# Loading the output projection's first four weight chunks ahead of the second stream's gated attention, with new load times in the planner

## The chip, the cores and the metric

The kernel runs on one NeuronCore of a Trainium2 chip. The metric is the device time of one execution in microseconds (us). TensorE multiplies matrices, VectorE and ScalarE work elementwise, GpSimd does a few small operations, and SyncE issues all the loads and stores, which 16 DMA engines carry out. In the rows these engines are PE (PEld for its weight loads), DVE, ACT, POOL and SP.

## The reference

Two transformer-like blocks follow each other on 256 tokens of width 1024, all in float32. The first block has two layers of feed-forward, token mixing and feed-forward. The second block carries two streams, the context `c` and the latent `x`, and its first layer is the place of the change:

```
yc, ctx_states = retention_gla_mixer(hc, ...)          # stream c, from zero states
y, _           = retention_gla_mixer(h, ..., ctx_states)   # stream x, from c's final states
y  = y  @ ev_w_out        # output projection, 1024 x 1024
yc = yc @ ev_w_out
x  = layer_norm(ALPHA * x  + g1  * y,  g, b)
xc = layer_norm(ALPHA * xc + cg1 * yc, g, b)
```

The mixer has two halves of 512 columns: retention with a fixed decay for each head, and gated linear attention (GLA), whose decays depend on the token. Each scans forwards and backwards. After the layer comes a multilayer perceptron for both streams, then a layer with window attention and a last perceptron.

## The kernel before

**Split products.** A float32 product is made of three matmuls: each operand is split into a rounded part (type fp32r) and the rest. For a weight chunk of 128 x 1024 numbers `wload` takes two tiles `r4` (the two parts) and one tile `f4` (the loaded chunk, 512 KB), lets SyncE load it, lets ScalarE cast it to the first part, and VectorE subtract to get the second. There are 30 `r4` tiles and 7 `f4` tiles. For the first two blocks of columns of each feed-forward of the first block, a chunk is loaded in two loads, one from the gate and one from the up matrix (`wide` with `W2`).

**The planner.** The kernel's functions do not emit instructions. They record operations in program order (`Plan.record`, line 165), with the tiles that they read and write, and a duration worked out from the shape. `Plan.schedule` (line 256) then simulates the engines and writes down an order: whenever an engine is free in the simulation, it takes the ready operation with the lowest rank (its place in program order, plus a delay for background work). That order is emitted for each engine, and on the chip each engine goes through its instructions in that order, each waiting for what it needs. So a planned duration that is wrong does not make the result wrong, but can put an instruction that has to wait ahead of one that need not.

Three rules of the planner matter here:

- A load's data is taken to be there some time after its issue (lines 402 to 405, below). Whoever depends on a load is ready from that time on. A second load into a tile which an earlier load was the first to write depends on that first load, too (line 209), although the two write different parts.
- SyncE may only take a load whose place is at most `AHEAD` = 200 operations behind the oldest operation that was not issued (line 380).
- A tile is handed out from a fixed number of slots for each tag. `can` (line 308) lets an operation take a slot out of program order only if every earlier allocation of that tag, not yet made, still has room. For this `take` adds one to the count of each of those earlier allocations; the count isn't lowered when the overtaking tile is free again.

```
if op.nbytes:
    end = avail[e] = t + 480.0
    dma_free = max(t + 1100.0, dma_free) + op.nbytes / DMA_RATE      # DMA_RATE = 360.0 bytes/ns
    fin = dma_free + 900.0
```

**The stage of the change.** `retention_gla` does the retention half for both streams, and then the GLA half: projections for both streams, and in a loop over `both` = (`c`, `x`) the scan of each. For each of two pairs of heads (`p`) and two directions (`dr`) it builds a table `E` of exponentials in an `f4` tile (matmul, then ScalarE's exponentials), multiplies queries and keys with it on VectorE (the last reader of `E` is the product for `q0`, a tile of tag `p`, in stream `x`), makes two banks of scores in `gu` tiles and two in `acc` tiles, copies them to `M` on ScalarE, and multiplies them with the values into two `acc` tiles. After stream `c`'s scan its final states go to an `f4` tile, and the gates of both streams are computed (`silu`, weight columns from 2560 on). `finish` normalizes each stream's outputs, applies the gate and splits them.

Then comes the output projection, in two halves of 512 columns (`half`, line 1811). It takes all four `acc` tiles, two for each stream. In the first half, chunk after chunk is loaded and multiplied for both streams; in the second half all four chunks are recorded first, then the products, and then layer norm and transposes. After that come the loads of the perceptron's first weights (`mlp_w`). Two `f4` tiles hold the context's residual through all of this. Gate and bias rows (`mod_...`) are computed in the background from weights in the tiles `mw` (loads from `in_ada_w` and `in_w_mod`), which VectorE sums up in the tiles `ma`.

Of the kernel before, what the change touches and what calls it, by code (L numbers as in the profile page):

```python
# [20 lines left out]
P = 128  # L21
# [5 lines left out]
ALPHA = 4.0 ** 0.25  # L27
# [14 lines left out]


class Op:
    __slots__ = ("eng", "fns", "dur", "nbytes", "deps", "succ", "allocs", "tiles", "prio", "idx", "table", "acc", "label", "rank", "cols")


class Clock:
# [3 lines left out]
    W = 4096 / 1.2  # L52
# [21 lines left out]
class Plan:  # L74
# [90 lines left out]
    def record(self, eng, fn, outs, ins, dur, nbytes=0, table=0, share=1.0):  # L165
        acc = []
        for aps, wr in ((ins, False), (outs, True)):
            for ap in aps:
                name = self.which(ap)
                if name is None:  # L170
                    continue
                tag = self.tag_of[name]
                if tag in PSUM_TAGS or tag == "dram":
                    acc.append((name, wr, 0, P, 1))
                else:
                    acc.append((name, wr, *self.region(ap)))
        last = self.ops[-1] if self.ops else None
        merge = (
            eng == "PE" and last is not None and last.eng == "PE" and last.dur + dur <= self.MERGE
            and {a[0] for a in acc if a[1]} == {a[0] for a in last.acc if a[1]}  # L180
        )
        if eng == "PE" and self.group is not None:
            merge = self.group == "all"
            self.group = "all"
        if merge:
            op = last
            op.fns.append(fn)
            op.dur += dur
            op.cols += dur * share
        else:  # L190
            op = Op()
            op.eng, op.fns, op.dur, op.nbytes, op.table = eng, [fn], dur, nbytes, table
            op.deps, op.succ, op.allocs, op.tiles, op.acc = set(), [], [], set(), []
            op.cols = dur * share
            op.idx = len(self.ops)
            op.label = self.label
            op.rank = op.idx + self.late
            self.ops.append(op)
        i = op.idx
        for name, wr, p0, p1, m in acc:  # L200
            h = self.hist.setdefault(name, [])
            for j, w2, q0, q1, m2 in h:
                if j != i and (wr or w2) and p0 < q1 and q0 < p1 and m & m2:
                    op.deps.add(j)
            if wr and name not in self.first:
                self.first[name] = i
                op.allocs.append(name)
            elif self.first.get(name, i) != i:
                op.deps.add(self.first[name])
            op.tiles.add(name)  # L210
        for a in acc:
            h = self.hist[a[0]]
            e = (i, *a[1:])
            if e not in h[-4:]:
                if a[1]:
                    h[:] = [x for x in h if not (a[2] <= x[2] and x[3] <= a[3] and (x[4] & ~a[4]) == 0 and x[0] != i)]
                h.append(e)
        op.acc.extend(acc)
# [37 lines left out]
    def schedule(self, verbose=False):  # L256
# [19 lines left out]
        ready_t = [0.0] * len(ops)  # L276
# [4 lines left out]
        dma_free = 0.0  # L281
# [55 lines left out]
        while n < len(ops):  # L337
# [13 lines left out]
            while progress:  # L351
                progress = False
                for e in self.ENGINES:
                    if avail[e] > t:
                        continue
                    admit(e, t)
                    best = None
                    for key, h in ready[e].items():
                        if not h:
                            continue  # L360

                        cand = h[0] if can(ops[h[0][1]]) else None
                        if cand is None and key:
                            for c in sorted(h)[:12]:
                                if can(ops[c[1]]):
                                    cand = c
                                    break
                            if cand is None:
                                for c in h:
                                    if can(ops[c[1]]):  # L370
                                        cand = c
                                        break
                        if cand is not None and (best is None or cand < best[0]):
                            best = (cand, key)
                    if best is None:
                        if waiting[e]:
                            heapq.heappush(events, waiting[e][0][0])
                        continue
                    (pr, i), key = best
                    if e == "SP" and i > oldest + self.AHEAD:  # L380
                        continue
                    h = ready[e][key]
                    if h[0] == (pr, i):
                        heapq.heappop(h)
                    else:
                        h.remove((pr, i))
                        heapq.heapify(h)
                    op = ops[i]
                    take(op)
                    dur = op.dur  # L390
                    if e == "ACT" and op.table and op.table != table and not (op.table == 3 and table in (1, 2)):
                        dur += 1300.0
                        table = op.table if op.table != 3 else 2
                    if e == "PE":
                        end = clock.run(t, dur, op.cols / dur)
                        dur = end - t
                    else:
                        end = t + dur
                    avail[e] = end
                    busy[e] += dur  # L400
                    fin = end
                    if op.nbytes:
                        end = avail[e] = t + 480.0
                        dma_free = max(t + 1100.0, dma_free) + op.nbytes / DMA_RATE
                        fin = dma_free + 900.0
                    seq.append(i)
                    issued[i] = True
                    while oldest < len(ops) and (issued[oldest] or ops[oldest].rank > oldest):
                        oldest += 1
                    self.start[i], self.end[i] = t, end  # L410
                    n += 1
                    heapq.heappush(events, end)
                    heapq.heappush(events, fin)
                    heapq.heappush(done, (fin, i))
                    for sx in op.succ:
                        o = ops[sx]
                        lat = (0.0 if op.nbytes else self.WRITE[e] + self.WAIT[o.eng]) if o.eng != e or op.nbytes else 0.0
                        ready_t[sx] = max(ready_t[sx], fin + lat)
                        ndep[sx] -= 1
                        if not ndep[sx]:  # L420
                            put(o)
                    progress = True
# [155 lines left out]
def two_blocks_kernel(ctx: ExitStack, tc: tile.TileContext, A: dict, out: bass.AP, dumps=None):  # L578
# [54 lines left out]
    def acc():  # L633
        return nc.tile("acc", 512, F32, 4)
# [277 lines left out]
    def kpairs(tiles):  # L912


        def f(k):
            c = slice((k % 2) * T, (k % 2) * T + T)
            return tiles[k // 2][0][:, c], tiles[k // 2][1][:, c]

        return f
# [5 lines left out]
    def kstream(tiles, n):  # L925


        def f(k):
            c = (k % 2) * 2 * T
            c = slice(c, c + 2 * T) if n is None else slice(c + n * T, c + n * T + T)  # L930
            return tiles[k // 2][0][:, c], tiles[k // 2][1][:, c]

        return f
# [568 lines left out]
    def retention_gla(nT, lgam, between):  # L1502
# [219 lines left out]
        S0 = None  # L1722
        for n in both:
            own = n == "c"
            po = [acc() for _ in range(2)]
            kd = [b2(), b2()] if own else None
            for p in range(2):
# [78 lines left out]
                S0 = states(kd, vb["c"], "g")  # L1806
                g = silu(2560)
            finish(n, po, g, ng)
        return {n: kpairs(y[n]) for n in both}

    def half(hid, W, k0, j, alpha, x, gates, tail, after=(), stats=None):


        order = [(n, t) for n in ("c", "x") for t in range(2)]
# [1 line left out]
        c = slice(j * 512, j * 512 + 512)  # L1816

        def chunk(i):
            k = (k0 + 2 * i) * P
            return wload(W[k : k + 2 * P, c].rearrange("(k p) c -> p k c", p=P), 2, 512)  # L1820

        def part(n, t, i, w):
            for k in range(2):
# [315 lines left out]
    x = {"c": hold["xc"], "x": xs}  # L2139
    both = ("c", "x")  # L2140
    nc.label = "ret"
    y = retention_gla({"c": kstream(sT, 0), "x": kstream(sT, 1), "both": kstream(sT, None)}, hold["lgam"], lambda: bg(1))

    def ln_tail(n, t, st, nxt, G, SH, g, b):
        mean, r = moments(st)
# [4 lines left out]
    get("Cg1_0", "Xg1_0")  # L2150
    gates = {n: V[n.upper() + "g1_0"] for n in both}
    stats = {(n, t): new_stats() for n in both for t in range(2)}
    half(y, A["ev_w_out_2"][0], 0, 0, ALPHA, x, gates, None, stats=stats)
    g, b = mod_row(A["ln_g_2"][0, 0]), mod_row(A["ln_b_2"][0, 0])
    nxt, maps = new_J(), {}
    for n in both:
# [128 lines left out]
```

## Time and profile before

| | |
|---|---|
| median of 3 runs | 2178.65 us (2177.21 to 2182.74) |
| the profiled execution's own time | 2175.03 us |
| its span, first to last instruction | 2173.3 us |
| busy: TensorE | 2082.8 us (96%) |
| busy: VectorE | 1592.1 us (73%) |
| busy: ScalarE | 994.3 us (46%) |
| mean granted TensorE clock, as a share of the full one | 0.986 |
| read from memory | 447.11 MB, 206 GB/s over the span |

A row of a timeline gives the start of a group of equal instructions, its length, the engine, the line, the operation with the tile written, the tiles read, sizes and the count; a bracket at its end gives how long the engine stood idle before it and what ended that. All instructions have one line, that of the recorder (L507), so they are told apart by their tiles: `f`, `r`, `b`, `p` are the tags `f4`, `r4`, `b2` and the small ones, `gu` and `acc` the accumulators. A row of a chain gives start, length, and what the time went to; a DMA there reaches from its issue to its landing.

### The profile page before, as it was taken

How to read it: one execution, taken by the hardware profiler on the slowest of the kernel's cores; microseconds unless marked ns; L12 is line 12 of the kernel's file. 1: busy time of each engine (PE TensorE's matmuls, PEld its weight loads, DVE VectorE, ACT ScalarE, POOL GpSimd, SP SyncE). 2: the span in 40 equal slices, each digit the busy share in tenths (PEclk: the TensorE clock that was granted, in tenths of full speed). 3: DMA queues.
4: the chain of work that ended last, by engine and by line, in shares of the span. 5: the costliest groups of instructions: out<-in, count | busy, mean ns of one | idle time of the engine just before them, and what ended most of it. 6: DMA issues, size and time to landing. Idle time of an engine off the chain costs nothing.

```text
span 2173.3 us, 33312 instructions
## 1 busy us (share of the span) xinstructions
PE 2082.8 (96%) x13124; PEld 1804.9 (83%) x13124; DVE 1592.1 (73%) x2115; ACT 994.3 (46%) x1527; POOL 52.4 (2%) x51
## 2 busy tenths in 40 slices
PE   7999899999999999999999899979999999999998
PEld 3899788889979998887998787768888888877997
DVE  6867898886687669899788866469754356888544
ACT  3644456454445445555544426333442331465551
POOL 0000000000000001000000000000000000000000
PEclk8999999999999999999999999999999999999999
DMA  9989867698869874686886544234742433144670
GB/s 340 369 276 322 269 207 264 223 298 272 269 224 314 260 259 149 211 264 213 277 299 229 167 149 141 87 127 140 246 156 91 137 115 102 68 156 146 204 222 30
DMA packets 273367, 450.51 MB, mean 207 GB/s; under 512 B 17677, under 2 KB 185773, under 8 KB 273209
## 3 DMA queue, kind: packets, MB, share of 16 engines
q1 hardware_dynamic: 273208, 448.37, 62.7%
q8 instruction: 103, 1.69, 0.3%
q14 instruction: 56, 0.45, 0.1%
HBM read 447.11 MB, written 1.20 MB: 206 GB/s over the span
## 4 chain that ended last, share of the span: by engine, by line
PE 66%; DVE 15%; DMA 11%; issue 3%; ACT 3%; POOL 0%; SPq 0%; DVEq 0%; ACTq 0%; POOLq 0%
PE gu L507 42%; PE acc L507 24%; DVE b L507 5%; DVE r L507 4%; DMA mw<-in_ada_w 3%; DVE ma L507 2%; DMA f<-in_ffn_wu 2%; DVE p L507 2%; ACT r L507 2%; DMA f<-in_ffn_wd 1%; DMA mw<-in_w_mod 1%; DVE resx L507 1%; DMA f<-in_w_in 1%; DMA f<-in_ev_w_out 1%; ACT b L507 1%
## 5 line engine op out<-in xcount | busy, mean ns | idle before, releaser
L507 PE MATMUL gu<-r,r 128*128 128x256 f32 (+2 forms) x8048 | 1197.8, 309 | 6.9 <-DVE r L507 3.8
L507 PEld LDWEIGHTS gu<-r,r 128*128 128x128 f32 (+1 forms) x8048 | 1093.3, 192 | 95.8 <-issue 12.0
L507 ACT CAST r<-f 128x1024 fp32r<-128x1024 f32 x545 | 564.3, 1051 | 538.8 <-PE acc L507 122.2
L507 DVE TENSOR_TENSOR r<-f,r 128x1024 fp32r<-128x1024 f32 x545 | 652.8, 1221 | 199.1 <-PE gu L507 73.2
L507 PE MATMUL acc<-r,r 128*128 128x512 f32 (+3 forms) x3264 | 724.1, 385 | 19.7 <-ACT b L507 11.6
L507 PEld LDWEIGHTS acc<-r,r 128*128 128x128 f32 (+1 forms) x3264 | 568.2, 189 | 142.8 <-ACT b L507 12.3
L507 DVE SCALAR_TENSOR_TENSOR ma<-mw,sc_all,ma 128x1024 f32<-128x1024 f32 x252 | 319.6, 1281 | 86.2 <-DMA mw<-in_ada_w 58.8
L507 ACT ACTIVATE b<-gu 128x512 f32<-128x512 f32 (+1 forms) x104 | 56.5, 554 | 143.6 <-PE gu L507 126.0
L507 DVE TENSOR_TENSOR r<-b,r 128x512 fp32r<-128x512 f32 (+1 forms) x74 | 46.0, 632 | 96.0 <-ACT r L507 95.9
L507 ACT CAST r<-gu 128x256 fp32r<-128x256 f32 (+2 forms) x130 | 42.9, 387 | 139.9 <-PE gu L507 139.9
L507 POOL TENSOR_TENSOR p<-p,mhalf 128x1 f32<-128x1 f32 (+2 forms) x42 | 49.7, 1188 | 2115.8 <-DVE p L507 2115.8
L507 PE MATMUL gu<-ident,b 128*128 128x128 f32 (+1 forms) x456 | 66.8, 292 | 33.2 <-DVE b L507 31.0
L507 PEld LDWEIGHTS gu<-ident,b 128*128 128x128 f32 (+1 forms) x456 | 49.8, 147 | 50.3 <-DVE b L507 43.4
L507 DVE TENSOR_TENSOR b<-acc,b 128x512 f32<-128x512 f32 (+1 forms) x82 | 54.9, 673 | 23.0 <-PE acc L507 21.2
L507 DVE TENSOR_TENSOR b<-b,b 128x512 f32<-128x512 f32 (+2 forms) x97 | 63.4, 667 | 6.9 <-PE acc L507 1.7
L507 ACT ACTIVATE ma<-mw,sc_all 128x1024 f32<-128x1024 f32 x36 | 41.5, 1152 | 49.1 <-DMA mw<-in_ada_w 25.6
L507 ACT ACTIVATE b<-acc,p 128x256 f32<-128x256 f32 (+1 forms) x96 | 51.5, 545 | 25.0 <-DVE p L507 20.9
L507 DVE TENSOR_TENSOR r<-gu,r 128x256 fp32r<-128x256 f32 (+2 forms) x130 | 49.5, 430 | 4.5 <-ACT r L507 4.2
L507 DVE SCALAR_TENSOR_TENSOR r<-b,r 128x512 fp32r<-128x512 f32 x44 | 30.3, 689 | 28.3 <-ACT r L507 28.1
L507 ACT CAST r<-b 128x512 fp32r<-128x512 f32 (+1 forms) x74 | 41.6, 573 | 11.8 <-DVE b L507 10.1
L507 DVE TENSOR_REDUCE p<-acc 128x2 f32<-128x512 f32 (+1 forms) x64 | 42.6, 684 | 3.3 <-PE acc L507 3.1
L507 ACT COPY b<-gu 128x512 f32<-128x512 f32 (+1 forms) x40 | 20.2, 525 | 52.0 <-PE gu L507 47.1
(122 smaller groups left out, 918.3 us busy)
## 6 DMA issues: line engine op xcount, KB each, us to landing
mw<-in_ada_w SPq DMA_DIRECT2D x128, 512.0 KB
f<-in_mlp_w SPq DMA_DIRECT2D x128, 512.0 KB
mw<-in_w_mod SPq DMA_DIRECT2D x96, 512.0 KB
f<-in_ffn_wd SPq DMA_DIRECT2D x88, 512.0 KB
f<-in_ffn_wg SPq DMA_DIRECT2D x72, 512.0 KB
f<-in_ffn_wu SPq DMA_DIRECT2D x72, 512.0 KB
f<-in_w_in SPq DMA_DIRECT2D x36, 512.0 KB
f<-in_w_gate SPq DMA_DIRECT2D x32, 512.0 KB
```

Of the source, the lines that this page charges most:

```text
L507: f(*[put(a) for a in args], **{k: put(a) for k, a in kw.items()})
```

## The change

It does three things. The first four chunks of the projection's first half (`out_chunk`) are recorded inside the GLA loop, at the start of stream `x`, and handed to `half` as `ready`. In the planner, a load into a tile that another load was the first to write, and with no overlap in what they write, is marked `soft`: it is ready when the first has been issued, not when it has landed. And the time from the end of a load's transfer to its landing is 1500 instead of 900 ns.

```diff
@@ record
             elif self.first.get(name, i) != i:
-                op.deps.add(self.first[name])
+                f = self.first[name]
+                if eng == "SP" and self.ops[f].eng == "SP" and f not in op.deps:
+                    op.soft.add(f)
+                op.deps.add(f)
             op.tiles.add(name)
+        op.soft &= op.deps
@@ schedule
                         dma_free = max(t + 1100.0, dma_free) + op.nbytes / DMA_RATE
-                        fin = dma_free + 900.0
+                        fin = dma_free + 1500.0
...
-                        ready_t[sx] = max(ready_t[sx], fin + lat)
+                        ready_t[sx] = max(ready_t[sx], end if i in o.soft else fin + lat)
@@ retention_gla
         for n in both:
             own = n == "c"
+            if not own:
+                first = [out_chunk(A["ev_w_out_2"][0], i, 0) for i in range(4)]
             po = [acc() for _ in range(2)]
...
-        return {n: kpairs(y[n]) for n in both}
+        return {n: kpairs(y[n]) for n in both}, first
+
+    def out_chunk(W, i, j):
+
+        return wload(W[2 * i * P : 2 * i * P + 2 * P, j * 512 : j * 512 + 512].rearrange("(k p) c -> p k c", p=P), 2, 512)
@@ half
-    def half(hid, W, k0, j, alpha, x, gates, tail, after=(), stats=None):
+    def half(hid, W, k0, j, alpha, x, gates, tail, after=(), stats=None, ready=None):
...
         def chunk(i):
-            k = (k0 + 2 * i) * P
-            return wload(W[k : k + 2 * P, c].rearrange("(k p) c -> p k c", p=P), 2, 512)
+            return ready[i] if ready else out_chunk(W, k0 // 2 + i, j)
@@ two_blocks_kernel
-    y = retention_gla(...)
+    y, first = retention_gla(...)
...
-    half(y, A["ev_w_out_2"][0], 0, 0, ALPHA, x, gates, None, stats=stats)
+    half(y, A["ev_w_out_2"][0], 0, 0, ALPHA, x, gates, None, stats=stats, ready=first)
```

## Rows read from the trace of the kernel before

**Rows 1.** The page, busy time of each engine, share of the span, instructions.
```profile
PE 2082.8 (96%) x13124; PEld 1804.9 (83%) x13124; DVE 1592.1 (73%) x2115; ACT 994.3 (46%) x1527; POOL 52.4 (2%) x51
```
**Rows 2.** Waits of TensorE from 1400 to 1520: total us, times, longest.
```profile
PE acc L507 <- ACT b L507: 8.8, 1, 8.8
```
**Rows 3.** Timeline of TensorE from 1310 to 1515.
```profile
1378.15 2.05 PE L507 MATMUL acc<-b,b 128*128 128x128 f32 x16 [1.60 <-DVE b L507]
...
1427.36 0.72 PE L507 MATMUL gu<-b 64*128 64x128 f32 x8 [0.84 <-DVE b L507]
...
1428.45 0.46 PE L507 MATMUL gu<-b,p 64*64 64x64 f32 x16
1437.73 2.93 PE L507 MATMUL acc<-r,r 128*128 128x512 f32 x6 [8.81 <-ACT b L507]
1440.46 1.06 PE L507 MATMUL acc<-b,b 128*128 128x128 f32 x4
...
1442.04 0.61 PE L507 MATMUL acc<-b,b 128*128 128x128 f32 x4
...
1442.85 1.64 PE L507 MATMUL acc<-r,r 128*128 128x512 f32 x6
```
**Rows 4.** Windows: length, busy by engine (count), clock, DMA share, GB/s.
```profile
1400.00:1405.00 5.00, 5.00 (x24) 4.13 (x23) 0.76 (x2) 0.66 (x2) 0.00 (x0) 1.00 0.00 0
...
1438.00:1440.00 2.00, 2.00 (x5) 1.56 (x6) 2.00 (x4) 1.67 (x2) 0.00 (x0) 0.50 0.05 20
...
1440.00:1460.00 20.00, 20.00 (x106) 17.32 (x105) 11.21 (x18) 3.54 (x7) 1.98 (x2) 0.95 0.40 114
```
**Rows 5.** Timeline of ScalarE from 1376 to 1470.
```profile
1413.11 0.60 ACT L507 ACTIVATE f<-gu 128x512 f32<-128x512 f32 x1 [0.68 <-PE gu L507]
...
1429.69 1.04 ACT L507 CAST r<-f 128x1024 fp32r<-128x1024 f32 x1 [4.23 <-DMA f<-in_ev_w_out]
...
1436.09 1.04 ACT L507 CAST r<-f 128x1024 fp32r<-128x1024 f32 x1 [4.09 <-DMA f<-in_ev_w_out]
1437.04 0.36 ACT L507 COPY b<-gu 128x256 f32<-128x256 f32 x1
...
1437.57 2.21 ACT L507 CAST r<-f 128x1024 fp32r<-128x1024 f32 x2
```
**Rows 6.** The chain that ended last, 1300 to 1520: start, us, what.
```profile
1381.49 5.67 DMA f<-in_ev_w_out
...
1428.61 7.41 DMA f<-in_ev_w_out
```
**Rows 7.** Timeline of SyncE's issues from 1340 to 1520.
```profile
1381.49 2.55 SPq L507 DMA_DIRECT2D f<-in_ev_w_out  x3
...
1417.66 9.38 SPq L507 DMA_DIRECT2D f<-in_ev_w_out  x4
...
1428.61 0.38 SPq L507 DMA_DIRECT2D f<-in_ev_w_out  x1
```
**Rows 8.** Waits of SyncE ending in 1416 to 1417.6: total us, times, longest.
```profile
SPq L507 <- DVE p L507: 21.6, 1, 21.6
```
**Rows 9.** Timeline of SyncE's issues from 0 to 70.
```profile
26.90 7.31 SPq L507 DMA_DIRECT2D f<-in_ffn_wg  x5
...
34.77 1.45 SPq L507 DMA_DIRECT2D f<-in_ffn_wu  x3
```
**Rows 10.** Timeline of TensorE from 0 to 66.
```profile
40.15 0.79 PE L507 MATMUL gu<-r,r 128*128 128x512 f32 x1 [2.24 <-ACT r L507]
42.10 9.97 PE L507 MATMUL gu<-r,r 128*128 128x512 f32 x35 [1.16 <-DVE r L507]
```
**Rows 11.** A window of the start, columns as in rows 4.
```profile
40.00:44.00 4.00, 2.69 (x6) 1.81 (x7) 4.00 (x4) 1.99 (x3) 0.00 (x0) 0.50 0.98 334
```
**Rows 12.** The chain and TensorE's timeline at the first feed-forward's end.
```profile
222.62 7.53 DMA mw<-in_ada_w
...
231.63 9.76 PE L507 MATMUL acc<-r,r 128*128 128x512 f32 x30 [4.74 <-ACT r L507]
```

More of the change, by code (lines that the diff above doesn't have):

```diff
@@ L44 @@
 class Op:
-    __slots__ = ("eng", "fns", "dur", "nbytes", "deps", "succ", "allocs", "tiles", "prio", "idx", "table", "acc", "label", "rank", "cols")
+    __slots__ = ("eng", "fns", "dur", "nbytes", "deps", "succ", "allocs", "tiles", "prio", "idx", "table", "acc", "label", "rank", "cols", "soft")
 class Clock:
@@ L193, in record @@
             op.deps, op.succ, op.allocs, op.tiles, op.acc = set(), [], [], set(), []
+            op.soft = set()
             op.cols = dur * share
@@ L2141, in two_blocks_kernel @@
     nc.label = "ret"
-    y = retention_gla({"c": kstream(sT, 0), "x": kstream(sT, 1), "both": kstream(sT, None)}, hold["lgam"], lambda: bg(1))
+    y, first = retention_gla({"c": kstream(sT, 0), "x": kstream(sT, 1), "both": kstream(sT, None)}, hold["lgam"], lambda: bg(1))
     def ln_tail(n, t, st, nxt, G, SH, g, b):
```

## The prediction

> **What bounds the kernel now.** I began with the busy shares. TensorE is busy for 2082.8 us, 96% of the span [rows 1]; only the rest, and stretches at a low clock, can be won. So the next view is what TensorE waits for. Its longest single wait, 8.8 us, is for ScalarE and lies on an accumulator of the output projection [rows 2]. The timeline shows the place. The last masks of the second stream's gated scan end at 1428.91 (1428.45 + 0.46), and the next matmul, of the projection, starts at 1437.73 [rows 3]. The reader should see three things there. The first six matmuls after the wait take 2.93 us; the same six take 1.64 us at 1442.85. The granted clock is 0.50 in 1438 to 1440 [rows 4], the lower of its two levels, 1.2 GHz, after TensorE had stood still for 8.8 us. And ScalarE did not lack input: the two copies which free the accumulators ran at 1437.04 and after, behind three casts of weight chunks, for which ScalarE waited 4.23 us and, at the last one, 4.09 us [rows 5]. ScalarE takes its instructions in the order written, so what held the copies was a load. The chain of waits names it: the load of `ev_w_out` issued at 1428.61, on its way for 7.41 us [rows 6].
>
> Why was it issued so late? Of the eight loads of this weight, three went out together from 1381.49, four between 1417.66 and 1427, and the last at 1428.61 [rows 7]. SyncE stood 21.6 us before 1417.66, waiting for a VectorE write to a `p` tile [rows 8]. In the code that is `q0`, the last reader of a gate table `E`. `can` lets a later tile overtake earlier ones of its tag only if every earlier one keeps room in the sequential order. Of the seven `f4` tiles the context residual holds two, the state matrix one and the running `E` one, so three loads may overtake the tables, and none more until they are handed out, even when the three are long done. From 1400 to 1405 DMA moved nothing, while ScalarE was busy 0.66 us of 5 and VectorE 0.76 us of 5 [rows 4].
>
> **Part 1, the four chunks.** The change records the first half's four loads, casts and subtractions ahead of the second stream's tables. They no longer overtake anything, and three loads of the second half may overtake instead. So seven of eight can be out before 1417, in the empty stretch, and one is left with the `mlp_w` loads. The four casts (1.04 us each) and four subtractions are moved, not added; they lie where ScalarE and VectorE are nearly idle. If that cover were gone they would cost at most 4 x 1.04 on ScalarE. On SyncE the four loads pass the loads of the gate rows and of one pair of `mw` tiles; those rows are first read after the scan. GpSimd issues none of these.
>
> With the last chunks in early, the copies follow the masks. How long TensorE then waits is not shown at this place; the bounds are 0 and 8.81. The nearest row is the same hand-over in the first stream's scan, 1.60 us [rows 3], and I take it: 8.81 - 1.60 = 7.2. The clock gives back 2.93 - 1.64 = 1.3 in the first six matmuls and 1.06 - 0.61 = 0.45 in the next four [rows 3]. Together 9.0 us. Does it last? From 1440 to 1460 VectorE is busy 11.21 of 20 us [rows 4], so it can take the next stage as much earlier. What is late next are the tables of the scan itself, where TensorE waited 0.84 us at most from 1419 on [rows 3].
>
> **Part 2, soft dependencies.** A second load into a tile that a load has opened is now planned when the first has been issued, not landed. That concerns the gate and up halves of the feed-forwards' first chunks, and small bias rows. At the start SyncE now issues five gate halves from 26.90 on and the first up half only at 34.77 [rows 9], so no chunk is whole before about 39. TensorE loses 2.24 and 1.16 us there [rows 10], and runs 2.69 us at the lower clock in 40 to 44 [rows 11], which costs half of that, 1.3. So the gain is at most 4.7. At the other end, VectorE is busy 4.00 of 4.00 us in that row, and DMA at 0.98 of its time, so an earlier half may only displace other work; a loss I bound by the next such wait, 4.74 at 226.89 [rows 12]. VectorE's row is the nearer one; I take a gain of 1.5.
>
> **Part 3, the load time.** The planner puts a 512 KB load's landing at 1.1 + 1.46 + 0.9 = 3.46 us after its issue on an empty queue, and now at 4.06. The chain's loads took 5.67 and 7.41 us [rows 6]. So the correction points the right way but closes only 0.6 of 2.2 to 4.0 us. No instruction is added; each order in which a cast stands near other work may flip. The wait that shows what a flip is worth is the one ending at 231.63, 4.74 us, where the chain runs through a load of 7.53 us [rows 12]. Bounds: one such wait gone, or one made elsewhere. I take 0, since 0.6 is small against 4.07 missing there. The page "SBUF — State Buffer" of the Trainium skill (section "The DMA setup-cost knee") gives a load a roughly fixed 2 us plus its bytes at an asymptote of 436 GB/s, by estimate 3.2 us here; by it the old figure was already high, this part would make the plan worse, and the late load would be worth 4.2 us less, so that the whole change gives 6.3 us and not 10.5. The trace disagrees with 5.67, 7.41 and 7.53 us, in stretches with several loads in flight.
>
> **The sum.** 9.0 + 1.5 + 0 = 10.5 us. Against the profiled execution's 2175.03 that is 2164.5. The median of the runs, 2178.65, lies 3.6 above that execution; I carry this over and predict 2168.
>
> **The rivals.**
> *The wait passes to the next load in line.* Once the projection's chunks are in, the loads of `mlp_w` take their slots, and the plan, still 1.6 us or more short, may put their casts before the copies. For it: two casts already stood between the two pairs of copies, and three of the four moved loads were early anyway. Against it: fewer loads are left after 1417, and one landing in time suffices. It gives part 2 alone, 2178.65 - 1.5 = 2177, give or take 4.7. Chance 0.20.
> *The casts come in front of the second stream's exponentials.* Those start at 1413.11 on ScalarE [rows 5] and open a chain where TensorE has little else. Three more loads may now go out just before, with their casts queued ahead. One issued before 1413.11 - 7.41 = 1405.7 is harmless; one issued at the end of the gap holds the whole scan by up to 7.41, and the clock falls again (1.75), while the old wait stays at the scan's end and the start wins nothing: 2178.65 + 9.2 = 2188. Against it: DMA is empty from 1400, so loads that may go, go early. Chance 0.11.
> *The old load time was right.* Then a cast at a change of stage is planned 0.6 too late; the kernel has eleven stages, so ten changes, 10 x 0.6 = 6.0: 2178.65 - 10.5 + 6.0 = 2174. This is what the page above would make of it. The 7.53 us load speaks against it. Chance 0.06.
> *More falls away than the one wait.* Part 2 gives its 4.7 and part 3 removes the 4.74: 2178.65 - 9.0 - 4.7 - 4.7 = 2160. Chance 0.13.
>
> **How the numbers follow.** The forecast has 0.50. About 0.3% (6.5 us) is what a measurement of this kernel can tell from no change. Faster by more: the forecast and the last rival, 0.63. Within: the first and the third, 0.26. Slower: 0.11. The range goes from the last rival's 2160 to 2180, the upper part of the first rival; it leaves out the slower case and the outer ends of the others, under 0.2.
>
> **What would show it.** Right: loads of `ev_w_out` between 1385 and 1413; no cast of them after about 1425; the wait at the projection's start under 2 us, and the clock at full level there; at the start gate and up halves alternate on SyncE, and TensorE's first feed-forward matmuls come before 40. Wrong: an 8 us wait for ScalarE still ahead of the projection, with `mlp_w` casts before it; or the exponentials waiting behind a cast; or new waits over 4 us at the ends of the feed-forwards, which would mean that the re-planned order, not the chunks, sets the result.

## The result and the profile after

| | before | after |
|---|---|---|
| median of four runs, same chip | 2180.69 us (2177.21 to 2183.47) | 2152.64 us (2148.30 to 2160.36) |
| profiled execution | 2175.03 us | 2160.36 us |
| its span | 2173.3 us | 2158.6 us |

The ratio is 0.9876, interval 0.9861 to 0.9892; the medians lie 28 us apart, where 10.5 were forecast, and the time is below the range's lower end of 2160. A reading note first: the two profiled executions lie only 14.7 us apart, since the one of before is 5.7 under its median and the one of after is the slowest of its four. So what follows finds about half of the gain in the traces, and the rest is between executions.

The page of the kernel after, its span and the busy line that answers to [rows 1].

```profile
span 2158.6 us, 33327 instructions
...
PE 2084.7 (97%) x13124; PEld 1807.8 (84%) x13124; DVE 1589.4 (74%) x2115; ACT 994.5 (46%) x1527; POOL 50.5 (2%) x51
```

The work of TensorE is the same, 13124 matmuls. Its idle time, span less busy, went from 2173.3 - 2082.8 = 90.5 us to 2158.6 - 2084.7 = 73.9. So 16.6 us of waits went, and the matmuls themselves took 1.9 us more. I use this difference as a yardstick for every kernel below; it is taken from one execution of each. What TensorE waited for over the whole span (total us, times, longest), first before:

```profile
PE gu L507 <- DVE b L507: 34.8, 26, 6.4
PE acc L507 <- ACT b L507: 11.6, 2, 8.8
PE acc L507 <- ACT r L507: 6.6, 3, 4.7
```

and after:

```profile
PE gu L512 <- DVE b L512: 32.8, 30, 6.6
...
PE acc L512 <- ACT r L512: 4.8, 2, 2.6
...
PE acc L512 <- ACT b L512: 2.6, 2, 2.3
```

The wait of the projection, 8.8 us, is the largest single one that went; the one at the first feed-forward's end, 4.7, went down too. The timeline of TensorE after shows both places, and what came new.

```profile
42.49 9.90 PE L512 MATMUL gu<-r,r 128*128 128x512 f32 x35 [2.44 <-DVE r L512]
...
228.48 0.73 PE L512 MATMUL acc<-r,r 128*128 128x512 f32 x2 [2.18 <-ACT r L512]
...
1372.93 2.98 PE L512 MATMUL acc<-b,b 128*128 128x128 f32 x16 [2.90 <-DVE b L512]
...
1422.88 0.46 PE L512 MATMUL gu<-b,p 64*64 64x64 f32 x16
1425.64 2.93 PE L512 MATMUL acc<-r,r 128*128 128x512 f32 x6 [2.30 <-ACT b L512]
1428.36 1.05 PE L512 MATMUL acc<-b,b 128*128 128x128 f32 x4
...
1431.63 1.75 PE L512 MATMUL acc<-r,r 128*128 128x512 f32 x6
```

Set the same instructions beside [rows 3]. The last masks start at 1422.88 and not 1428.45, so 5.57 us were won before the gated scan ended. The projection starts at 1425.64 and not 1437.73, 12.09 earlier, so the shorter wait (8.81 to 2.30) gave 6.5 there. The remaining 2.6 of the 14.7 us lie behind. The first six matmuls after the wait still take 2.93 us, and so the clock still fell: the windows of after (columns as in rows 4) have 0.50, as before, up to 1432.

```profile
1426.00:1428.00 2.00, 2.00 (x6) 1.52 (x6) 0.65 (x2) 0.00 (x0) 0.00 (x0) 0.50 0.19 57
1428.00:1430.00 2.00, 2.00 (x10) 1.90 (x9) 0.00 (x0) 0.00 (x0) 0.00 (x0) 0.50 0.00 0
1430.00:1432.00 2.00, 2.00 (x11) 2.00 (x10) 0.43 (x1) 0.65 (x2) 0.00 (x0) 0.53 0.00 0
1432.00:1434.00 2.00, 2.00 (x14) 1.73 (x14) 0.01 (x1) 0.00 (x0) 0.00 (x0) 1.00 0.00 0
```

At 1372.93 a wait that was 1.60 us [rows 3] is now 2.90, and the same 16 matmuls take 2.98 us and not 2.05: a piece given back.

The timeline of SyncE's issues after answers to [rows 7, 9].

```profile
28.03 0.38 SPq L512 DMA_DIRECT2D f<-in_ffn_wg  x1
28.64 0.38 SPq L512 DMA_DIRECT2D f<-in_ffn_wu  x1
...
1368.88 8.78 SPq L512 DMA_DIRECT2D f<-in_ev_w_out  x4
...
1381.77 3.54 SPq L512 DMA_DIRECT2D f<-in_ev_w_out  x3
...
1412.03 0.38 SPq L512 DMA_DIRECT2D f<-in_ev_w_out  x1
1413.77 6.82 SPq L512 DMA_DIRECT2D f<-in_mlp_w  x2
```

And that of ScalarE after to [rows 5].

```profile
1407.47 0.60 ACT L512 ACTIVATE f<-gu 128x512 f32<-128x512 f32 x1 [0.68 <-PE gu L512]
...
1423.99 1.04 ACT L512 CAST r<-f 128x1024 fp32r<-128x1024 f32 x1 [4.11 <-DMA f<-in_mlp_w]
1424.94 0.37 ACT L512 COPY b<-gu 128x256 f32<-128x256 f32 x1
```

Seven of eight chunks are out early and one is left, as the prediction said; four go out from 1368.88 and three from 1381.77, even ahead of its 1385 to 1413. The exponentials at 1407.47 wait no longer than in [rows 5]. But a cast still stands in front of the copies that free the accumulators: now one of `mlp_w`, for which ScalarE waits 4.11 us, and TensorE behind it 2.30.

### The profile page after: what moved, and what is told of

Its sections match the earlier page's. It is cut to its first block, busy times and chain, and to the rows that moved or that the text cites. A ratio compares the mean times of both kernels' runs of the same rounds, so it can differ in the third digit from the quotient of the medians.

```text
span 2158.6 us, 33327 instructions
## 1 busy us (share of the span) xinstructions
PE 2084.7 (97%) x13124; PEld 1807.8 (84%) x13124; DVE 1589.4 (74%) x2115; ACT 994.5 (46%) x1527; POOL 50.5 (2%) x51
## 3 DMA queue, kind: packets, MB, share of 16 engines
q1 hardware_dynamic: 273208, 448.37, 63.4%
## 4 chain that ended last, share of the span: by engine, by line
PE 68%; DVE 19%; DMA 7%; issue 3%; ACT 1%; POOL 1%; SPq 0%; DVEq 0%; ACTq 0%; POOLq 0%
PE gu L512 44%; PE acc L512 24%; DVE b L512 6%; DVE r L512 5%; DVE ma L512 3%; DVE p L512 2%; DMA f<-in_ffn_wu 2%; DMA mw<-in_ada_w 1%; DMA f<-in_w_gate 1%; DVE resx L512 1%; DMA f<-in_w_in 1%; ACT r L512 1%; POOL p L512 1%; DMA f<-in_w_o 0%; DVE f L512 0%
## 5 line engine op out<-in xcount | busy, mean ns | idle before, releaser
L512 ACT ACTIVATE r<-b 128x512 fp32r<-128x512 f32 x44 | 27.7, 629 | 41.1 <-DVE b L512 40.7
```

Of the source, the lines that this page charges most:

```text
L512: f(*[put(a) for a in args], **{k: put(a) for k, a in kw.items()})
```

## The experiments

The question was which part made 28 us out of 10.5. The kernels differ from the kernel before in the planner's inputs or in where the four chunks are recorded, and so in the order of the same work. Each ratio is against the kernel before on the same chip. Idle is the yardstick above (profiled execution); the last column is TensorE's wait ahead of the projection. Where I say the n-th matmul, matmuls are counted from the start of each trace, and the start of the n-th is compared; all traces have 13124.

| kernel | median us | ratio [interval] | idle us | wait us |
|---|---|---|---|---|
| before | 2180.6 to 2182.6 | 1 | 90.5 | 8.81 |
| chunks alone | 2174.50 | 0.9969 [0.9956, 0.9981] | 84.6 | 2.13 |
| soft dependencies alone | 2187.79 | 1.0026 [1.0011, 1.0040] | 100.6 | 8.98 |
| load time 1500 alone | 2155.95 | 0.9887 [0.9870, 0.9904] | 76.9 | 4.61 |
| soft and 1500, no chunks | 2154.37 | 0.9881 [0.9864, 0.9899] | 73.7 | 4.15 |
| the whole change | 2152.64 | 0.9876 [0.9861, 0.9892] | 73.9 | 2.30 |
| 1200 alone | 2167.88 | 0.9937 [0.9922, 0.9952] | 81.9 | 4.86 |
| 1490 alone | 2156.59 | 0.9889 [0.9874, 0.9904] | 75.3 | 3.90 |
| 2500 alone | 2152.28 | 0.9874 [0.9860, 0.9889] | 72.4 | 3.38 |
| 4000 alone | 2157.21 | 0.9888 [0.9872, 0.9905] | 80.9 | 0.79 |
| 1500 for `f4` chunks only | 2169.44 | 0.9945 [0.9926, 0.9963] | 84.0 | 4.71 |
| 1500 for `mw` tiles only | 2170.23 | 0.9948 [0.9930, 0.9966] | 82.5 | 8.03 |
| chunks and 2500 | 2148.37 | 0.9845 [0.9824, 0.9867] | 66.7 | 2.79 |
| whole change with 2500 | 2141.01 | 0.9815 [0.9800, 0.9830] | 63.4 | 2.94 |

**The parts, one at a time.** First the four chunks without the rest of the change.

```diff
+            if not own:
+                first = [out_chunk(A["ev_w_out_2"][0], i, 0) for i in range(4)]
...
```

> The four chunks alone, with the old load time and no soft dependencies. Theory A (the chunks carry the gain: the accumulators' copies no longer wait behind late weight casts): the wait ahead of the output projection falls from 8.8 us to about 2.3, and the kernel gains 6 to 9 us, about 2172 against 2181. Theory B (the load time carries it, at the ends of all stages): the old planned time still puts the next loads' casts ahead of the copies, the wait stays above 6 us, and the gain is under 3 us. Theory C (any edit deals the whole order anew, and the gain is the luck of one order): waits change in stages long before the edit, and the median may lie anywhere within 10 us of 2181.

0.9969 is 0.0031 x 2182.6 = 6.8 us, within the 6 to 9 of theory A. The timeline of TensorE:

```profile
1382.85 2.64 PE L510 MATMUL acc<-b,b 128*128 128x128 f32 x16 [2.92 <-DVE b L510]
...
1433.04 0.46 PE L510 MATMUL gu<-b,p 64*64 64x64 f32 x16
1435.64 2.93 PE L510 MATMUL acc<-r,r 128*128 128x512 f32 x6 [2.13 <-ACT b L510]
```

The wait fell by 8.81 - 2.13 = 6.7 us, and the six matmuls still take 2.93; the next four take 0.80, 1.06 before. The part does what it should for the wait, and next to nothing for the clock. But in this trace the masks start at 1433.04, 4.6 us later than in [rows 3], and the hand-over of the first stream waits 2.92 and not 1.60: other places lost, and the projection starts only 2.1 us earlier. So the trace shows the wait, and the gain of the whole kernel rests on the medians.

The soft dependencies without the rest:

```diff
...
+                if eng == "SP" and self.ops[f].eng == "SP" and f not in op.deps:
+                    op.soft.add(f)
...
-                        ready_t[sx] = max(ready_t[sx], fin + lat)
+                        ready_t[sx] = max(ready_t[sx], end if i in o.soft else fin + lat)
```

> The soft dependencies alone. Theories A and B: gate and up halves alternate at the start as in the full change, the first feed-forward matmuls still come at about 42 since VectorE is full there, the wait of 8.8 us stays; 0 to 2 us gained, 2179 to 2181. Theory C: waits change in many stages, and the median may lie anywhere within 10 us of 2181.

Slower by 0.0026 x 2182.6 = 5.7 us (2.4 to 8.7 by the interval), where theories A and B had 0 to 2 us gained. The timeline of TensorE:

```profile
37.70 0.47 PE L512 MATMUL gu<-r,r 128*128 128x512 f32 x1
40.95 10.54 PE L512 MATMUL gu<-r,r 128*128 128x512 f32 x35 [2.77 <-DVE r L512]
...
233.07 9.04 PE L512 MATMUL acc<-r,r 128*128 128x512 f32 x30 [7.63 <-ACT r L512]
...
1451.66 2.93 PE L512 MATMUL acc<-r,r 128*128 128x512 f32 x6 [8.98 <-ACT b L512]
```

At the start the part does what was forecast. The first feed-forward's matmuls come earlier than in [rows 10], and the 401st matmul starts at 99.43, 1.5 us before the 100.89 of the kernel before. The lead is lost at the first feed-forward's end, where the wait grew from 4.74 [rows 12] to 7.63. The timeline of VectorE there:

```profile
230.35 1.28 DVE L512 SCALAR_TENSOR_TENSOR ma<-mw,sc_all,ma 128x1024 f32<-128x1024 f32 x1 [3.90 <-DMA mw<-in_ada_w]
```

Before, the same sum ran at 228.91, after a wait of 4.02 for its load (its line stands below, with the load time). So TensorE comes to the place 1.5 us earlier and waits longer for a load that lands 1.4 us later; it is 1.4 behind after it. At the masks (1442.22) it is 13.8 us behind [rows 3], and the projection kept its own wait. At which places the rest was lost is not shown.

The load time without the rest:

```diff
-                        fin = dma_free + 900.0
+                        fin = dma_free + 1500.0
```

> The load time of 1500 instead of 900 alone. Theory A: a few us at most, 2176 to 2181. Theory B: most of the gain of 28 us, about 2160, with TensorE's waits at the ends of the feed-forwards shorter. Theory C: within 10 us of 2181, and the waits that went are others than in the full change.

This one number brings 0.0113 x 2182.6 = 24.7 us by the ratio, 26.7 by the medians: nearly all of the whole change, as theory B had it. Its page:

```profile
span 2155.4 us, 33324 instructions
...
PE 2078.5 (96%) x13124; PEld 1800.6 (84%) x13124; DVE 1590.6 (74%) x2115; ACT 995.0 (46%) x1527; POOL 51.4 (2%) x51
```

Of the 17.9 us between the spans, 90.5 - 76.9 = 13.6 are idle time and 2082.8 - 2078.5 = 4.3 are matmuls that ran in less time. (The other 8.8 of the 26.7 lie between executions again: before's profiled one is 7.6 under this chip's median, this one 1.2 above its own.) How a planner's figure does that is to be seen at the projection, where this kernel changed no chunk. SyncE's issues there:

```profile
1404.88 9.37 SPq L510 DMA_DIRECT2D f<-in_ev_w_out  x4
```

The timeline of ScalarE:

```profile
1416.83 1.04 ACT L510 CAST r<-f 128x1024 fp32r<-128x1024 f32 x1 [4.16 <-DMA f<-in_ev_w_out]
1419.10 1.04 ACT L510 CAST r<-f 128x1024 fp32r<-128x1024 f32 x1 [1.22 <-DMA f<-in_ev_w_out]
1420.05 0.37 ACT L510 COPY b<-gu 128x256 f32<-128x256 f32 x1
...
1423.66 1.04 ACT L510 CAST r<-f 128x1024 fp32r<-128x1024 f32 x1 [2.98 <-DMA f<-in_ev_w_out]
```

And of TensorE, with three earlier places ahead of it:

```profile
43.91 0.79 PE L510 MATMUL gu<-r,r 128*128 128x512 f32 x1 [2.96 <-ACT r L510]
...
233.24 0.73 PE L510 MATMUL acc<-r,r 128*128 128x512 f32 x2 [2.12 <-ACT r L510]
...
1002.50 0.66 PE L510 MATMUL gu<-ident,b 128*128 128x128 f32 x4 [3.25 <-DVE b L510]
...
1415.67 0.46 PE L510 MATMUL gu<-b,p 64*64 64x64 f32 x16
1420.74 2.93 PE L510 MATMUL acc<-r,r 128*128 128x512 f32 x6 [4.61 <-ACT b L510]
...
1429.20 0.71 PE L510 MATMUL acc<-b,b 128*128 128x128 f32 x4 [2.00 <-DVE b L510]
```

The loads still go out late, from 1404.88 on, and ScalarE still waits for three of them. But the last of the three casts, in [rows 5] ahead of the copies, now stands behind them. ScalarE loses 2.98 us for that load as well, only after it has handed TensorE its accumulators. TensorE waits 4.61 and not 8.81 us. Of these 4.2 us, 2.0 come back at 1429.20, where the kernel before has no wait. At the first feed-forward's end the wait is shorter, too. VectorE's timeline there before:

```profile
228.91 1.28 DVE L507 SCALAR_TENSOR_TENSOR ma<-mw,sc_all,ma 128x1024 f32<-128x1024 f32 x1 [4.02 <-DMA mw<-in_ada_w]
230.23 0.69 DVE L507 TENSOR_TENSOR b<-b,gu 128x512 f32<-128x512 f32 x1
```

With 1500 it is:

```profile
229.81 1.23 DVE L510 TENSOR_TENSOR r<-f,r 128x1024 fp32r<-128x1024 f32 x1 [1.08 <-ACT r L510]
231.07 0.69 DVE L510 TENSOR_TENSOR b<-b,gu 128x512 f32<-128x512 f32 x1
```

No sum over an `mw` tile, with a load of its own to wait for, stands directly ahead of `b<-b,gu` any more, and TensorE's wait there is 2.12 us, 4.74 before. That is no gain of 2.6 us, though. Ahead of `b<-b,gu` stands now a subtraction of a weight chunk, whose cast waited 6.85 us for its load. And TensorE comes to the place 4.2 us later than before (its wait begins at 231.12 and not at 226.89), since this kernel is late from the start: its first feed-forward matmul runs at 43.91, against 40.15 in [rows 10]. After the wait it is still 1.6 us behind, and 30 matmuls on, with 28 of them in 6.64 us where before all 30 took 9.76, it is level. The lead is won later. The row that answers to 1002.50 is before

```profile
1010.23 0.66 PE L507 MATMUL gu<-ident,b 128*128 128x128 f32 x4 [3.70 <-DVE b L507]
```

Both are the 6521st matmul, so there 1500 alone is 7.7 us ahead. At the masks it is 12.78 [rows 3], at the projection's first matmul 17.0, at the end 17.9. The gain was gathered in pieces of a few us along the whole kernel, most of it ahead of the projection.

**Without the chunks.** The soft dependencies and 1500, the chunks left where they were. Against the kernel after:

```diff
-            if not own:
-                first = [out_chunk(A["ev_w_out_2"][0], i, 0) for i in range(4)]
+            first = None
```

> The whole change without its four chunks (soft dependencies and load time stay). Theory A: it loses the 6 to 9 us of the projection's wait against the full change, so about 2160. Theory B: nearly the full gain, about 2155, as the load time alone makes the copies come before late casts. Theory C: not the sum of its parts run alone; anywhere within 10 us of 2165.

2154.37 us, and with the chunks 2152.64: 0.9876 / 0.9881 = 0.9995, give or take 0.0024. So beside the new load time the chunks bring at most 0.3%, and perhaps nothing, though the wait at the projection falls from 4.15 to 2.30.

**Luck, or a price?** A planner may turn over many orders at any small change. If 1500 had hit a lucky one, 1490 would lose it, and 1200 need not lie between.

```diff
-                        fin = dma_free + 900.0
+                        fin = dma_free + 1490.0
```

> The load time of 1490 instead of 1500 ns, no chunks, no soft dependencies: ten nanoseconds mean nothing for the match between plan and chip. Theory B (a planned landing nearer the real one keeps late casts away from the work in hand): as with 1500, 2156, within 4 us. Theory C (one lucky order): more than 6 us away from 2156, toward 2181.

The same line with 1200.0:

> The load time of 1200, half of the step. Theory B: between before's 2181 and 2156, about 2165 to 2172. Theory C: unrelated to the step, anywhere from 2150 to 2190.

With 2500.0:

> The load time of 2500, so a 512 KB load is planned to land 5.06 us after its issue, near the 5.67 us of a chain's load. Theory B: a further gain, 2140 to 2150, with TensorE's waits at the ends of the feed-forwards shorter again. Rival (past 1500 the plan only puts casts later than they need be): 2156 to 2170. Theory C: anywhere.

And with 4000.0:

> The load time of 4000, so a load is planned to land 6.56 us after its issue, above 5.67 and below 7.5 us of the slow ones. Theory B: about as 2500, 2140 to 2155. Rival (casts too late): TensorE waits for casts (ScalarE r) at the stage changes and the time is above 2165. Theory C: anywhere.

The gain is 0.63% at 1200, 1.11% at 1490, 1.13% at 1500, 1.26% at 2500 and 1.12% at 4000: it grows with the step and then stays, which one lucky order at 1500 would not do. From 1490 to 4000 the intervals overlap, so the top is flat as far as these runs tell. 1200 and 1490 came as theory B had them. At 2500 neither the further gain (2140 to 2150) nor the loss (2156 to 2170) is there, and 4000 lies between its two expectations.

At 4000 few loads come too late (ScalarE's waits for them, summed over its list, fall from 362 us before to 127), but idle is 80.9 us and not 72.4 as at 2500. One of TensorE's waits there:

```profile
PE gu L510 <- DVE ma L510: 7.7, 1, 7.7
```

It has no like in the list of before. I read it as the other side of the same price: work planned for a landing later than the real one stands behind work that could have come after it. That is a reading and was not shown. At the projection 4000 does what no other kernel here does:

```profile
1411.78 1.67 PE L510 MATMUL acc<-r,r 128*128 128x512 f32 x6 [0.79 <-ACT b L510]
...
1420.26 2.93 PE L510 MATMUL acc<-r,r 128*128 128x512 f32 x6 [3.64 <-ACT b L510]
```

The wait ahead of it is 0.79 us and the clock stays up. The stop comes nine us later, 3.64 us long, at the next pair of copies, again behind casts that wait for `ev_w_out`.

**Which loads?** 1500 for the weight chunks alone, then for the `mw` tiles of the background alone.

```diff
-                        fin = dma_free + 900.0
+                        fin = dma_free + (1500.0 if any(self.tag_of[x] == "f4" for x in op.tiles) else 900.0)
```

> 1500 ns for the loads of weight chunks (tiles f4) alone, 900 for all others; no chunks ahead, no soft dependencies. If late weight casts on ScalarE and subtractions on VectorE are what held other work: most of the 25 us, 2156 to 2163. If late background loads (mw, summed on VectorE) are: under a third of it, 2173 to 2181. If both matter in like parts: 2164 to 2172.

```diff
-                        fin = dma_free + 900.0
+                        fin = dma_free + (1500.0 if any(self.tag_of[x] == "mw" for x in op.tiles) else 900.0)
```

> 1500 ns for the background weights' loads (tiles mw) alone. Weights theory: 2173 to 2181. Background theory: 2156 to 2163. Both in like parts: 2164 to 2172; and with the run before it the two gains add up to about 25 us.

0.55% and 0.52%, in sum 1.07% against 1.13% for both, as the theory of like parts had it. Neither ScalarE's casts nor VectorE's sums are the cause alone. With `mw` alone the projection's wait stays, 8.03 us, as it should: what holds ScalarE there is a weight chunk.

**A better version?** The chunks with 2500, and the whole change with 2500. In both the planner's line is, against the kernel before:

```diff
-                        fin = dma_free + 900.0
+                        fin = dma_free + 2500.0
```

> The chunks ahead with the load time of 2500, no soft dependencies. If the chunks still buy what they do alone (about 7 us) on a plan with good load times: about 2145. If the load time has taken the same wait away already: 2150 to 2156, as with 2500 alone.

> The whole change with 2500 instead of 1500. If its three parts are independent: 2140 to 2148, better than both kernels. If load time and chunks take away the same waits and the soft dependencies are worth nothing: 2148 to 2156, within 4 us of the change itself.

The whole change with 2500 takes 2141.01 us (2138.47 to 2142.22): 39.8 us under the kernel before on its chip, and its ratio lies wholly under that of the change as made (0.9861 at the least). It came as expected for independent parts; the chunks with 2500 came between their two expectations. The 6.4 us wait for `b` at the start of the second block, which neither the change nor 1500 alone had touched (6.6 and 6.5 at the longest), looks gone from its list of waits: the longest for `b` is 2.5. The timeline shows that it was split.

```profile
1201.66 0.66 PE L512 MATMUL gu<-ident,b 128*128 128x128 f32 x4 [2.53 <-DVE b L512]
...
1207.04 2.50 PE L512 MATMUL gu<-r,r 128*128 128x512 f32 x5 [4.49 <-DVE r L512]
```

The two together are 7.0 us, and 2500 alone has the same pair (2.53 and 4.48). At 2500 the chunks bring 0.9845 / 0.9874 = 0.9971, and the soft dependencies on top 0.9815 / 0.9845 = 0.9970, each give or take 0.0027, so both gains are only just clear of zero. (The runs with and without the soft dependencies are from one chip and do not overlap: 2138.47 to 2142.22 against 2143.83 to 2150.90.)

## Why the prediction was right in direction and far too small

**What bounds the kernel** held: what was won came out of TensorE's waits and, in part, its clock (in 1500 alone 13.6 us of idle time and 4.3 of matmul time), and the projection's wait came from casts queued ahead of copies on ScalarE.

**Part 1, the chunks, 9.0 us.** Measured alone: 6.8. The wait went to 2.13, where 1.60 was taken; that term stands at 6.7 against 7.2. Of the 1.75 for the clock 0.26 came back in this kernel (four matmuls in 0.80 and not 1.06) and nothing in the kernel after. The hand-over from which I took 1.60 keeps the clock up (16 matmuls in 2.05 us); the stops of 2.13 and 2.30 did not (six in 2.93). Two of my signs failed with it: the wait is not under 2 us, and the clock is not at full level. I had taken the clock's term as sure once the long stop was gone, and priced only that side of it.

**Part 2, soft dependencies, +1.5 us.** Measured alone: a loss of 5.7. The term itself came true at the start: gate and up halves alternate on SyncE, the first feed-forward matmul comes at 37.70 (39.28 in the kernel after, whose transposes just ahead of it start 1.6 later than before), and the lead is 1.5 us at the 401st matmul. What failed is that I priced only the start and one such wait against it. The lead was eaten at the first feed-forward's end, where the load that TensorE's work stands behind did not come earlier, and more was lost at later places.

**Part 3, the load time, 0 us.** This is the step that failed: "I take 0, since 0.6 is small against 4.07 missing there". It measured 24.7 to 26.7 us. The whole change was forecast at 10.5 and measured at 28, so this term is more than the whole miss of 17.5; parts 1 and 2 came out 2.2 and 7.2 lower than forecast. Two things were wrong in it. A figure that closes 0.6 us of a gap of 4 does not have to close it. Where it is enough to put one late cast behind a copy, as at the projection, TensorE is spared about the whole real wait for that load: 4.2 us there for 0.6 of correction (ScalarE's stall was 4.09 [rows 5]), even if 2.0 came back at the next copies. The size of that flip is the size of the stall that changed place. And I bounded the part by one wait of 4.74 us although I wrote that "each order in which a cast stands near other work may flip", and counted ten changes of stage for the opposite rival. Ten such places at the price of one wait bound the gain at some 47 us; the runs showed about half of that.

**The rivals.** That the wait passes to the next load in line was true in small: the cast of `mlp_w` at 1423.99 takes the place of the old one, for 2.30 us and not 8.8. That casts hold the exponentials did not happen (0.68 us, as before). That the old load time was right is excluded by 1200, 1490 and 1500, each faster than 900. By the Trainium skill's page "SBUF — State Buffer", section "The DMA setup-cost knee" (a fixed 2 us or so, and the bytes at 436 GB/s), I had estimated 3.2 us for a chunk's load. The runs do not agree: the plan is better with 4.06 us (1500) than with 3.46, and in the whole change better still with 5.06 (2500). That more falls away than the one wait was the right story, with chance 0.13, but with one wait of 4.74 as its price it stopped at 2160.

**The carry-over.** I added 3.6 us for before's profiled execution standing under its median. For the change the sign was the other way: its profiled execution stands 7.7 us above its median. This is scatter of single executions and nothing to carry.

**Left open.** Multiplied, the three parts alone give 0.9969 x 1.0026 x 0.9887 = 0.9882, which agrees with 0.9876. But the soft dependencies cost 0.26% at 900 and bring 0.30% at 2500, and why is not shown. It is not only the start: the whole change with 2500 leads the chunks with 2500 by 3.2 us at the 401st matmul (99.02 against 102.25), by 0.9 at the 4401st (689.94, 690.86) and by 8.1 at the 8729th (1352.34, 1360.48). Nor was it shown which instructions changed places along the kernel: that a late load stopped standing in front of TensorE's work is shown at the projection alone, and for the rest of the gain it is inferred from the sweep and from the two kinds of loads.

## What to carry to other kernels

On engines that run in written order, a planner's time for a load decides what stands behind the stall, so an optimistic figure makes unrelated work wait: set it by the loads' measured times and sweep it, before moving single loads by hand (here 4.06 to 5.06 us served well, where single loads took 5.67 to 7.53, and 6.56 was no better). Price such a figure by the stalls that it can move, at all places where one is planned near work that TensorE waits for, not by the size of the correction. And judge a part alone and beside the others: here one part lost alone and gained with the right load time.

## What the runs showed that was not expected

The total time that ScalarE waits for loads fell by only a tenth with 1500 alone (362 us before, 326 after, by its list of waits), and VectorE's not at all (107.5 and 107.7), while the kernel gained 25 us. At 4000 ScalarE's fell to 127, and the kernel is no faster than at 1500. So how long an engine waits for loads did not set the time; that what is queued behind it does is shown at the projection.

In the kernel after, the stop of 2.30 us left the clock as low as the one of 8.81 had (0.50, 0.50 and 0.53 from 1426 to 1432, then 1.00). So the short wait costs 2.93 - 1.64 = 1.3 us more in the first six matmuls alone. With 4000, after a stop of 0.79, the same six take 1.67 (granted clock 1.00 from 1411 to 1416).

One and the same kernel, the one after, took between 2148.30 and 2160.36 us, with mean granted clocks from 0.990 to 0.985 in the same order at the two ends. A 12 us scatter between executions is more than most single steps of this study, so differences of two profiles tell where, and the medians how much.
